# Modulation sums over the partitions: plain fp32, unsplit, the columns halved over the output partitions

## The chip, the cores and the metric

The kernel runs on one core of a Trainium2 chip. Its time is the device time of one execution in microseconds. The kernel before took 1994.59 us (median of three runs, 1993.12 to 1994.67). A profile is one further execution, recorded instruction by instruction; its times begin at the first instruction. Engines are named as in the profile: PE is TensorE (PEld its weight loads), ACT is ScalarE, DVE is VectorE, POOL is GpSimd and SP is the queue that issues most transfers.

## The reference, cut to what matters

One decoder layer on 256 tokens of 2048 channels, all in fp32: an FFN, a mixer (pooling and attention, gated) and a second FFN. Each of the three is modulated by nine vectors that come from the conditioning vector `c`:

```
mod = (silu(c) @ w_ada + b_ada).reshape(9, 2048)      # w_ada: 2048 x 18432
h = rms_norm(x, g) * (1 + mod[1]) + mod[0];  x = x + 0.5 * mod[2] * swiglu(h, ...)   # first FFN
h = rms_norm(x, g) * (1 + mod[4]) + mod[3];  x = x + mod[5] * (merged @ w_o)         # mixer
h = rms_norm(x, g) * (1 + mod[7]) + mod[6];  x = x + 0.5 * mod[8] * swiglu(h, ...)   # second FFN
```

So three of the vectors are shifts, three are scales and three (numbers 2, 5 and 8) are gates.

## The kernel before

**The weight products.** Activations are held transposed, with channels on the 128 partitions and tokens as columns. Each large product has a piece of the activations as its stationary operand (128x128) and 512 weight columns as its moving operand, and sums over the channels in a PSUM bank. Both operands are split into a high and a low half of the type fp32r, and three of the four products are formed (`mm`, the matmuls on L304): 12 matmuls for 128 channels, 1024 columns and both blocks of tokens. The weights are split on the chip as they arrive: ScalarE casts the high half (`wh`, L285, three buffers) and VectorE subtracts it (`wl`, L289).

**Turns.** The order of the work is written out by hand. One "turn" is the matmuls of one weight piece. `push` puts a piece's matmuls off until two more pieces have been prepared (`LAG` is 2), and `at(n, f)` puts `f` behind the matmuls of turn `n`. The planner `spread` places work of a given cost into turns that have room, by the costs booked with `will`; a booked cost changes where later work lands, not the work itself. `hop(n, f, g, early)` puts `f` into turn `n` and `g` into the next, and moves both on past turns at which a column set ends. The eight PSUM banks are two groups of four: one holds the running column set, and `bank()` hands out the other four in turn for all else.

**The modulation sums.** The first two vectors are made at the start, in another way. The other seven are made by `ada_plan`, in 15 blocks spread over the three stages: 13 of 1024 columns and 2 of 512. For one block, VectorE multiplies each piece of `w_ada` (128 rows) by the matching column of silu(c) and adds it to an accumulator `acc` of 128 partitions (L230, 16 operations). The sum over the 128 partitions is then left, and `sums` does it for 512 columns at a time, 28 times in all:

- `halves`, one turn after the last accumulation: ScalarE casts the high half of `acc` (L189), VectorE subtracts for the low half (L190). Both go into buffers of the tag `t2`, of which there are three.
- `prod`, two turns later: two matmuls with a matrix of ones as the stationary operand (L195, L196) give the sums, alike on all 128 output partitions of a bank.
- `use`, in the next turn: for a gate, ScalarE writes the 512 columns into the gate's tile, scaled (L202). For a shift or a scale, `mod_col` takes them to one column for each 128 channels: VectorE multiplies by the identity (L168), reduces (L171) and adds the bias (L175 to L178).

`halves` is booked at 0.65 and `mod_col` at 1.7. The second 512 columns of a block follow the first at least two turns later. The next block starts in the turn in which the last accumulation of the one before stands.

Of the kernel before, what the change touches and what calls it, by code (L numbers as in the profile page):

```python
# [9 lines left out]
F32 = mybir.dt.float32  # L10
F32R = mybir.dt.float32r
BF16 = mybir.dt.bfloat16
AF = mybir.ActivationFunctionType
ALU = mybir.AluOpType
AX = mybir.AxisListType

P = 128
# [12 lines left out]
CW = 512  # L30
# [4 lines left out]
T2 = 3  # L35
# [8 lines left out]
def trunk_layer(ctx, tc, x, c, w_ada, b_ada, g_ffn1, w_ffn1_gu, w_ffn1_down, g_mix, w_in,  # L44
                pool_mix, pool_scale, w_pool_up, q_gain, k_gain, sinks, rel_bias, w_attn_up,
                w_o, g_ffn2, w_ffn2_gu, w_ffn2_down, pool_w, onehot, out):
    nc = tc.nc
    pool = lambda name, bufs=1, **kw: ctx.enter_context(tc.tile_pool(name=name, bufs=bufs, **kw))
    const = pool("const")
# [5 lines left out]
    def nm(s):  # L55
        uid[0] += 1
        return f"{s}_{uid[0]}"

    def t_(shape, tag, bufs=1, dt=F32):
        return sb.tile(list(shape), dt, tag=tag, bufs=bufs, name=nm(tag))  # L60
# [5 lines left out]
    def bank_at(i, shape):  # L66
        return ps.tile(list(shape), F32, tag=f"bank{i}", name=nm("bank"))

    def bank(shape=(P, CW)):
        for _ in range(4):  # L70
            rr[0] = (rr[0] + 1) % 4
            i = (1 - cur[0]) * 4 + rr[0]
            if i not in held:
                return bank_at(i, shape)
        raise RuntimeError("no bank free in the written order")


    ident = const.tile([P, P], F32, name="ident")
    make_identity(nc, ident)
    ones_f = const.tile([P, P], F32, name="ones_f")  # L80
    nc.gpsimd.memset(ones_f, 1.0)
    ones = const.tile([P, P], F32R, name="ones")
    nc.vector.tensor_copy(ones, ones_f)

    x_sb = const.tile([P, T, D], F32, name="x_sb")

# [29 lines left out]
    def at(n, f, first=False):  # L116

        fs = plan.setdefault(max(n, done[0]), [])
        fs.insert(0, f) if first else fs.append(f)
# [4 lines left out]
    def hop(n, f, g, early=0):  # L124


        while n in ends or early > 0 and n + 1 in ends or early > 1 and n - 1 in ends:
            n += 1
        at(n, f)
        at(n + 1, g)  # L130
        return n
# [11 lines left out]
    def spread(n, m, cost, cap=9.0):  # L143

        out, left = [], 0.0
        while len(out) < m:
            r = room.get(n, ROOM)
            left = min(left, 2 * cost) + max(0.0, min(r - busy.get(n, 0.0), r * cap / ROOM))
            while left >= cost and len(out) < m:
                out.append(n)  # L150
                left -= cost
            n += 1
        return out

    def will(n, t):
        busy[n] = busy.get(n, 0.0) + t
# [5 lines left out]
    gates = {}  # L162

    def mod_col(j, b, c0):

        k, n = c0 // P, b.shape[1] // P
        d = t_([P, n, P], "t2", T2)
        nc.vector.tensor_tensor(d, b.rearrange("p (a q) -> p a q", a=n),  # L168
                                ident.unsqueeze(1).to_broadcast([P, n, P]), ALU.mult)
        m = mcol[:, j, k:k + n]  # L170
        nc.vector.tensor_reduce(m, d, AX.X, ALU.add)  # L171
        i, o = j // 3, j % 3
        bc = bcol[:, (2 * i + o) * KD + k:(2 * i + o) * KD + k + n]
        if o == 0:
            nc.vector.tensor_tensor(m, m, bc, ALU.add)  # L175
        else:
            nc.vector.scalar_tensor_tensor(out=m, in0=m, scalar=1.0, in1=bc, op0=ALU.add, op1=ALU.add)
            nc.vector.tensor_tensor(m, m, gcol[:, i * KD + k:i * KD + k + n], ALU.mult)  # L178

    def ada_plan(js, n0, cap=9.0):  # L180

        def sums(j, c0, a, n, o):
            got = []

            def halves():
                hi, lo = t_([P, CW], "t2", T2, F32R), t_([P, CW], "t2", T2, F32R)
                nc.scalar.copy(hi, a[0][:, o:o + CW])  # L189
                nc.vector.tensor_tensor(lo, a[0][:, o:o + CW], hi.bitcast(F32), ALU.subtract)  # L190
                got.extend((hi, lo))

            def prod():
                got.append(bank())
                nc.tensor.matmul(got[2], ones, got[0], start=True, stop=False)  # L195
                nc.tensor.matmul(got[2], ones, got[1], start=False, stop=True)  # L196

            def use():
                if j % 3 == 2:
                    if j not in gates:  # L200
                        gates[j] = t_([P, D], "gate", 1)
                    nc.scalar.activation(gates[j][:, c0 + o:c0 + o + CW], got[2], AF.Copy, scale=1.0 if j == 5 else 0.5)  # L202
                else:
                    mod_col(j, got[2], c0 + o)

            at(n, halves)
            q = hop(n + 2, prod, use, 2)
            will(n, 0.65)
            if j % 3 != 2:
                will(q + 1, 1.7)  # L210
            return q

        for j, c0, a_w in js:
            a, r, nk = [], [], 2 * SW // a_w
            where = spread(n0, KD, 1.24 * a_w / SW, cap)
            for kk, n in enumerate(where):
                def go(j=j, c0=c0, kk=kk, a=a, r=r, w=a_w, nk=nk):
                    if kk == 0:
                        a.append(t_([P, w], "acc", 2))
                        if j % 3 == 2:  # L220
                            nc.gpsimd.memset(a[0], 0.0)
                            nc.gpsimd.dma_start(a[0][0:1, :], b_ada[0:1, j * D + c0:j * D + c0 + w])
                    if kk % nk == 0:
                        r[:] = [t_([P, nk, w], "raw", RAW)]
                        nc.sync.dma_start(r[0], ada_v[:, kk:kk + nk, j * D + c0:j * D + c0 + w])
                    sc = cs[:, kk:kk + 1]
                    if kk == 0 and j % 3 != 2:
                        nc.vector.tensor_scalar_mul(a[0], r[0][:, 0, :], sc)
                    else:
                        nc.vector.scalar_tensor_tensor(out=a[0], in0=r[0][:, kk % nk, :], scalar=sc, in1=a[0],  # L230
                                                       op0=ALU.mult, op1=ALU.add)
                at(n, go)
                will(n, 1.24 * a_w / SW)
            n0 = n
            q = n
            for i in range(a_w // CW):
                q = sums(j, c0, a, max(n + 1 + 2 * i, q + 1), i * CW)


    class Set:  # L240
# [309 lines left out]
    def ffn(w_gu, w_down, hh, hl, actT, f0, sg, g, jgate, after, js):  # L550
# [25 lines left out]
        for i in range(4):  # L576
            will(n + KF - 1 + 2 * i, 1.36)
        ada_plan(js, pushed[0], ROWS)
        while f0 < DFF:
            fw = min(SW, DFF - f0)  # L580
# [41 lines left out]
    for i, g in enumerate((g_ffn1, g_mix, g_ffn2, pool_scale)):  # L622
        n = g.shape[1] // P
# [132 lines left out]
    b = bank_at(4, (P, KG + KB))  # L756
# [48 lines left out]
    for k, n, need in ((2, 4, 14), (6, 4, 42), (10, 4, 70), (14, 2, 74)):  # L805
# [29 lines left out]
        q = k  # L835
        while q < k + n:
            m = 1 if q == k + n - 1 else 2
            if q - q % 2 in xT:
                at(e + (q > k + 1), lambda q=q, m=m: h_pair(xT[q - q % 2][:, q % 2:q % 2 + m, :], q, m))
            else:  # L840
                xn, o = [], (q - k) // 2
# [9 lines left out]
    for i, k0, k1 in segs:  # L851
        s = Set(w_ffn1_gu[0], KD, cols[i], hstat, late=True)
        if n0 == 0:
# [3 lines left out]
            h = t_([P, 2, S], "t2", T2)  # L857
# [213 lines left out]
    for a in range(0, 8, 2):  # L1071
        with_bank(G[0] + 1 + a // 4, (P, 2, S), pool_prod(a),
                  lambda b, a=a: nc.vector.tensor_copy(pT_[0][:, a:a + 2, :], b))
        will(G[0] + 2 + a // 4, 0.7)
    for a in range(8):
        with_bank(G[0] + 4 + a // 2, (P, S), mix_prod(a),
                  lambda b, a=a: nc.scalar.activation(mixT[:, a, :], b, AF.Copy, scale=psc[:, a:a + 1]))
# [100 lines left out]
    for g, n in enumerate((2, 5, 9, 13, 17, 22, 25, 28)):  # L1178
        heads(G[0] + n, g)
    ada_plan([(j, c, SW) for j in (5, 6) for c in (0, SW)] + [(7, CW, CW), (7, SW, SW)], nQ)  # L1180

    tk = [(t, i) for t in range(T) for i in range(2)]
# [19 lines left out]
    for half_ in range(2):  # L1202
        c0 = half_ * SW
# [55 lines left out]
    g, hh, hl = transition(s, SW, 5, 6, lambda stat: Set(w_ffn2_gu[0], KD, (0, SW), stat, flip=False, late=True))  # L1259
# [76 lines left out]
```

## Time and profile before

| | |
|---|---|
| median of three runs | 1994.59 us |
| the profiled execution's own time | 1996.08 us |
| its span, first to last instruction | 1994.3 us |
| TensorE, matmuls | 1972.3 us busy, 8873 records |
| TensorE, weight loads | 1629.3 us busy |
| VectorE | 1513.6 us busy, 1749 instructions |
| ScalarE | 1091.8 us busy, 1484 instructions |
| matmuls of the modulation sums (L195 and L196) | 28 records each |
| splits of the accumulators (L189 on ScalarE, L190 on VectorE) | 28 each, 17.3 and 19.2 us busy |
| gate writes (L202) | 12, 7.1 us busy |
| granted TensorE clock, mean | 0.996 |

A row of the timeline has the start and the time from the first start to the last end in microseconds, the engine, the line and operation, the tile written and those read, the shape, and how many instructions stand together. A matmul's end is modelled and overlaps its follower, so starts are compared with starts. A row of a group has, behind the bar, the busy microseconds, the mean nanoseconds of one, and behind the second bar the engine's idle time just before, with what ended it. A matmul's shape is first that of its stationary operand (128\*64 is 128 rows and 64 columns), then that of its moving operand. In the table by stretches each engine has its busy time and number of instructions (PE, PEld, DVE, ACT, POOL), and then come the granted clock, the busy share of the DMA engines and GB/s.

### The profile page before, as it was taken

The page shows a single profiled execution, that of the slowest core. Times are in us where ns is not written, and L with a number is a line of the kernel's source. Part 1 is how long each engine was busy: PE and PEld are TensorE (multiplying, and loading weights), DVE is VectorE, ACT ScalarE, POOL GpSimd, SP SyncE. Part 2 cuts the span into 40 slices and gives each one's busy share as a digit, 9 for nine tenths or more (in the row PEclk, how much of TensorE's full clock was granted, in tenths as well). Part 3 has the DMA queues.
Part 4 walks back from the last instruction along what each step waited for, and adds up shares of the span by engine and source line. Part 5 has one row for each costly group of instructions (what it writes and reads, how often), then busy time and mean ns, then how long its engine had stood idle before and what let it go on. Part 6 is the DMA issues. An engine that isn't in the chain of part 4 may idle for free.

```text
span 1994.3 us, 23770 instructions
## 1 busy us (share of the span) xinstructions
PE 1972.3 (99%) x8873; PEld 1629.3 (82%) x8873; DVE 1513.6 (76%) x1749; ACT 1091.8 (55%) x1484; POOL 26.4 (1%) x51
## 2 busy tenths in 40 slices
PE   7999999999999999999999999999999999999999
PEld 6788888888788888888788888888888888888887
DVE  6898867989999978886889998888455454565655
ACT  6543457664664546446656455645564645565443
POOL 0000000000000000000000000000000000000000
PEclk9999999999999999999999999999999999999999
DMA  9989745899899966876688996598555645466652
GB/s 364 371 314 342 261 164 187 329 337 356 313 363 336 335 230 235 310 281 219 235 292 302 351 311 219 212 356 317 214 189 202 219 170 190 159 225 216 218 185 74
DMA packets 158212, 523.68 MB, mean 263 GB/s; under 512 B 9325, under 2 KB 21509, under 8 KB 157840
## 3 DMA queue, kind: packets, MB, share of 16 engines
q1 hardware_dynamic: 156464, 518.83, 72.7%
q0 software_dynamic: 1632, 3.34, 0.6%
q8 instruction: 69, 1.13, 0.2%
q14 instruction: 47, 0.39, 0.1%
HBM read 520.00 MB, written 2.12 MB: 262 GB/s over the span
## 4 chain that ended last, share of the span: by engine, by line
PE 96%; DVE 2%; DMA 1%; SPq 0%; issue 0%; ACT 0%; DVEq 0%; ACTq 0%
PE bank L304 93%; DVE acc L662 1%; DMA raw<-in_w_ffn_gu_dram 1%; DMA raw<-in_w_ada_dram 0%; DVE wl L289 0%; PE bank L1065 0%; SPq L654 0%; PE bank L820 0%; PE bank L196 0%; PE bank L195 0%; PE bank L357 0%; PE bank L1128 0%; PE bank L1092 0%; PE bank L999 0%; PE bank L1051 0%
## 5 line engine op out<-in xcount | busy, mean ns | idle before, releaser
L285 ACT CAST wh<-raw 128x1024 fp32r<-128x1024 f32 (+2 forms) x711 | 711.1, 1002 | 793.9 <-PE bank L304 739.7
L289 DVE TENSOR_TENSOR wl<-raw,wh 128x1024 fp32r<-128x1024 f32 (+2 forms) x713 | 823.5, 1157 | 418.4 <-ACT wh L285 413.7
L304 PE MATMUL bank<-wh,hl 128*128 128x512 f32 (+1 forms) x2088 | 653.6, 388 | 0.0
L304 PE MATMUL bank<-wh,hh 128*128 128x512 f32 (+1 forms) x2064 | 651.3, 390 | 0.3 <-DVE big L1099 0.3
L304 PE MATMUL bank<-wl,hh 128*128 128x512 f32 (+1 forms) x2064 | 647.5, 389 | 0.6 <-DVE wl L289 0.6
L304 PEld LDWEIGHTS bank<-wh,hl 128*128 128x128 f32 x2088 | 392.7, 188 | 81.3
L304 PEld LDWEIGHTS bank<-wl,hh 128*128 128x128 f32 x2064 | 388.2, 188 | 82.9 <-DVE wl L289 2.9
L304 PEld LDWEIGHTS bank<-wh,hh 128*128 128x128 f32 x2064 | 386.4, 189 | 80.2 <-issue 0.8
L230 DVE SCALAR_TENSOR_TENSOR acc<-raw,cs,acc 128x1024 f32<-128x1024 f32 (+1 forms) x231 | 279.8, 1211 | 0.8
L304 PE MATMUL bank<-wh,sh 128*128 128x512 f32 x656 | 203.7, 390 | 0.0
L304 PE MATMUL bank<-wh,sl 128*128 128x512 f32 x656 | 203.3, 389 | 0.0
L304 PE MATMUL bank<-wl,sh 128*128 128x512 f32 x656 | 203.1, 389 | 0.0
L304 PEld LDWEIGHTS bank<-wh,sl 128*128 128x128 f32 x656 | 123.0, 188 | 26.0 <-DVE sl L394 0.3
L304 PEld LDWEIGHTS bank<-wl,sh 128*128 128x128 f32 x656 | 123.1, 188 | 25.8
L304 PEld LDWEIGHTS bank<-wh,sh 128*128 128x128 f32 x656 | 122.6, 188 | 25.8 <-issue 0.4
L542 ACT COPY big<-raw 32x512 f32<-32x512 f32 (+1 forms) x208 | 121.9, 586 | 4.2
L662 DVE SCALAR_TENSOR_TENSOR acc<-raw,cs,acc 128x1024 f32<-128x1024 f32 (+2 forms) x74 | 77.7, 1052 | 1.0
L394 DVE TENSOR_TENSOR sl<-big,sh 128x512 fp32r<-128x512 f32 x82 | 56.2, 686 | 0.0
L393 ACT CAST sh<-big 128x512 fp32r<-128x512 f32 x82 | 50.7, 618 | 0.0
L784 DVE TENSOR_TENSOR big<-bank,big 128x512 f32<-128x512 f32 x56 | 36.4, 684 | 0.0
L329 ACT ACTIVATE junk<-x_sb 128x512 bf16<-128x512 f32 x24 | 15.2, 632 | 13.9 <-DVE x_sb L421 11.7
L538 DVE STREAM_TRANSPOSE raw<-sg 128x1024 f32<-128x1024 f32 (+1 forms) x20 | 22.7, 1133 | 0.0
(220 smaller groups left out, 802.7 us busy)
## 6 DMA issues: line engine op xcount, KB each, us to landing
raw<-in_w_ffn_gu_dram SPq DMA_DIRECT2D x175, 1024.0 KB, 5.3
raw<-in_w_ada_dram SPq DMA_DIRECT2D x112, 1024.0 KB, 7.2
raw<-in_w_ffn_down_dram SPq DMA_DIRECT2D x86, 1024.0 KB, 6.1
raw<-in_w_in_dram SPq DMA_DIRECT2D x48, 1024.0 KB, 6.8
raw<-in_w_ada_dram SPq DMA_DIRECT2D x64, 512.0 KB, 7.6
raw<-in_w_o_dram SPq DMA_DIRECT2D x15, 1024.0 KB, 7.8
raw<-in_w_pool_up_dram SPq DMA_DIRECT2D x8, 1024.0 KB, 7.9
raw<-in_w_attn_up_dram SPq DMA_DIRECT2D x8, 1024.0 KB, 6.9
```

Of the source, the lines that this page charges most:

```text
L230: nc.vector.scalar_tensor_tensor(out=a[0], in0=r[0][:, kk % nk, :], scalar=sc, in1=a[0], op0=ALU.mult, op1=ALU.add)
L285: nc.scalar.copy(wh, raw_k)
L289: nc.vector.tensor_tensor(wl[:, e], raw_k[:, e], wh[:, e].bitcast(F32), ALU.subtract)
L304: nc.tensor.matmul(self.banks[t][i], a[:, sl], w[:, o], start=first and q == 0, stop=last and q == 2)
L329: nc.scalar.activation(junk, x_sb[:, t, n * CW:(n + 1) * CW], AF.Square, scale=(D / 2) ** -0.5, accum_out=ssq[:, t, n:n + 1])
L393: nc.scalar.copy(hi, src[:, k:k + n, :])
L394: nc.vector.tensor_tensor(lo, src[:, k:k + n, :], hi.bitcast(F32), ALU.subtract)
L538: nc.vector.transpose(z[0][:, t, :], (src() if callable(src) else src)[:, t, 0:n])
L542: nc.scalar.copy(actT[32 * j:32 * j + 32, k:k + m, :].rearrange("p k (t i r) -> p k t i r", t=T, i=4)[:, :, :, i, :], z[0][32 * i:32 * i + ...
L662: nc.vector.scalar_tensor_tensor(out=acc, in0=r, scalar=sc, in1=acc, op0=ALU.mult, op1=ALU.add)
L784: nc.vector.tensor_tensor(a, b, a, ALU.add)
```

## The change

A block's sum over the partitions is formed in one go, for all of its columns, from the unsplit fp32 accumulator. There are two plain fp32 matmuls with 64 columns of ones: one sums one half of the block's columns into output partitions 0 to 63, the other sums the other half into partitions 64 to 127 of the same bank. For a gate the halves are the first and the last columns of the block; for a shift or scale they are the first and the last 64 of every 128. `halves` is gone. `prod` stands two turns after the last accumulation instead of three.

For a shift or a scale, `mod_col` works once on a bank of 512 columns for a block of 1024 (256 for one of 512), with a 128x64 pattern `ident2`, the two halves of the identity added, in place of the identity. For a gate, each half is written twice, once to either half of the gate's partitions: four ScalarE operations of 64 partitions. Of the costs booked, 0.65 is gone and 1.7 for 512 columns becomes 1.4 for a block of 1024 columns (0.75 for one of 512).

```
@@ -79,8 +79,8 @@
     make_identity(nc, ident)
     ones_f = const.tile([P, P], F32, name="ones_f")
     nc.gpsimd.memset(ones_f, 1.0)
-    ones = const.tile([P, P], F32R, name="ones")
-    nc.vector.tensor_copy(ones, ones_f)
+    ident2 = const.tile([P, 64], F32, name="ident2")
+    nc.vector.tensor_tensor(ident2, ident[:, 0:64], ident[:, 64:P], ALU.add)
 
     x_sb = const.tile([P, T, D], F32, name="x_sb")
 
@@ -163,10 +163,11 @@
 
     def mod_col(j, b, c0):
 
-        k, n = c0 // P, b.shape[1] // P
-        d = t_([P, n, P], "t2", T2)
+
+        k, n = c0 // P, 2 * b.shape[1] // P
+        d = t_([P, n, 64], "t2", T2)
         nc.vector.tensor_tensor(d, b.rearrange("p (a q) -> p a q", a=n),
-                                ident.unsqueeze(1).to_broadcast([P, n, P]), ALU.mult)
+                                ident2.unsqueeze(1).to_broadcast([P, n, 64]), ALU.mult)
         m = mcol[:, j, k:k + n]
         nc.vector.tensor_reduce(m, d, AX.X, ALU.add)
         i, o = j // 3, j % 3
@@ -181,34 +182,34 @@
 
 
 
-        def sums(j, c0, a, n, o):
+        def sums(j, c0, a, n, w):
             got = []
 
-            def halves():
-                hi, lo = t_([P, CW], "t2", T2, F32R), t_([P, CW], "t2", T2, F32R)
-                nc.scalar.copy(hi, a[0][:, o:o + CW])
-                nc.vector.tensor_tensor(lo, a[0][:, o:o + CW], hi.bitcast(F32), ALU.subtract)
-                got.extend((hi, lo))
-
             def prod():
-                got.append(bank())
-                nc.tensor.matmul(got[2], ones, got[0], start=True, stop=False)
-                nc.tensor.matmul(got[2], ones, got[1], start=False, stop=True)
+
+                got.append(bank((P, w)))
+                for g in range(2):
+                    if j % 3 == 2:
+                        m = a[0][:, g * w:(g + 1) * w]
+                    else:
+                        m = a[0].rearrange("p (a h r) -> p a h r", h=2, r=64)[:, :, g, :]
+                    nc.tensor.matmul(got[0][64 * g:64 * g + 64], ones_f[:, 0:64], m, start=True, stop=True)
 
             def use():
                 if j % 3 == 2:
                     if j not in gates:
                         gates[j] = t_([P, D], "gate", 1)
-                    nc.scalar.activation(gates[j][:, c0 + o:c0 + o + CW], got[2], AF.Copy, scale=1.0 if j == 5 else 0.5)
+                    for g in range(2):
+                        c_ = c0 + g * w
+                        for r in range(0, P, 64):
+                            nc.scalar.activation(gates[j][r:r + 64, c_:c_ + w], got[0][64 * g:64 * g + 64],
+                                                 AF.Copy, scale=1.0 if j == 5 else 0.5)
                 else:
-                    mod_col(j, got[2], c0 + o)
-
-            at(n, halves)
-            q = hop(n + 2, prod, use, 2)
-            will(n, 0.65)
+                    mod_col(j, got[0], c0)
+
+            q = hop(n, prod, use, 2)
             if j % 3 != 2:
-                will(q + 1, 1.7)
-            return q
+                will(q + 1, 0.1 + 1.3 * w / CW)
 
         for j, c0, a_w in js:
             a, r, nk = [], [], 2 * SW // a_w
@@ -232,9 +233,7 @@
                 at(n, go)
                 will(n, 1.24 * a_w / SW)
             n0 = n
-            q = n
-            for i in range(a_w // CW):
-                q = sums(j, c0, a, max(n + 1 + 2 * i, q + 1), i * CW)
+            sums(j, c0, a, n + 2, a_w // 2)
 
 
     class Set:
```

## The prediction

> **What bounds the kernel now.** I read the page first, for the busy shares.
>
> ```profile
> PE 1972.3 (99%) x8873; PEld 1629.3 (82%) x8873; DVE 1513.6 (76%) x1749; ACT 1091.8 (55%) x1484; POOL 26.4 (1%) x51
> ```
>
> TensorE has no room: 8873 matmul records in a span of 1994.3 us. A busy share can overstate a pipelined engine, so the chain of waits in order of time came next. Its longest piece is the last quarter of the kernel.
>
> ```profile
> 1415.51 573.96 PE bank L304 x2532
> ```
>
> There the chain is nothing but weight matmuls (L304), each starting 573.96 / 2532 = 0.2267 us after the one before. This is the pace of the kernel wherever nothing interrupts it; every microsecond put into or taken out of TensorE's queue moves the end by as much. The view of waits says who waits for whom.
>
> ```profile
> ACT wh L285 <- PE bank L304: 739.7, 544, 5.4
> ```
>
> ScalarE's casts of the weights wait 739.7 us in total for TensorE to free their buffers: the preparing engines run ahead and are held back by TensorE. Work taken off ScalarE or VectorE is worth nothing except where TensorE is caught waiting for them. So the change is priced in TensorE's queue first, and then at the places where it waits.
>
> **The change, part by part.** The kernel makes 15 blocks of modulation sums inside the three big stages: 13 of 1024 columns and 2 of 512, by the lists handed to the planner.
>
> *Removed: the fp32r product.* Each 512 columns have two matmuls (L195, L196), one for either half of the split. TensorE's timeline around one such sum:
>
> ```profile
> 414.19 0.39 PE L304 MATMUL bank<-wh,hl 128*128 128x512 f32 x1
> 414.42 0.62 PE L304 MATMUL bank<-wl,hh 128*128 128x512 f32 x2
> 414.88 0.39 PE L195 MATMUL bank<-t,ones 128*128 128x512 f32 x1
> 415.11 0.40 PE L196 MATMUL bank<-t,ones 128*128 128x512 f32 x1
> 415.34 0.62 PE L304 MATMUL bank<-wh,hh 128*128 128x512 f32 x2
> 415.80 0.39 PE L304 MATMUL bank<-wh,hl 128*128 128x512 f32 x1
> ```
>
> From 414.19 to 415.80 are 1.61 us with five L304 starts and the sum: 1.61 - 5 x 0.2267 = 0.48 us for a sum. There are 28, so 0.96 us for a wide block, 0.48 us for a narrow one, and 13.4 us in all.
>
> *Added: two plain fp32 matmuls a block, one to either half of the output partitions.* No sum in the trace has that form, but two neighbours do. A full-width plain fp32 product is L1065, of 256 columns:
>
> ```profile
> 895.96 1.89 PE L1065 MATMUL bank<-sg,raw 128*128 128x256 f32 x8
> 897.50 0.58 PE L195 MATMUL bank<-t,ones 128*128 128x512 f32 x1
> 897.92 0.40 PE L196 MATMUL bank<-t,ones 128*128 128x512 f32 x1
> 898.16 0.63 PE L304 MATMUL bank<-wh,hh 128*128 128x512 f32 x2
> ```
>
> From 895.96 to 898.16 are 2.20 us; without the sum's 0.48 that is 1.72 us for 8 records, 0.215 us each. That is nearly the 0.2267 us of an L304 record with twice the columns, so a plain fp32 record costs 1.9 times as much per column. I take 0.43 us for 512 columns. Plain fp32 also doubles the records. The attention's output product (L1161) has 8 calls in the code, one to either half of the partitions for each of four groups of heads and one of the two blocks, and the groups of matmuls show 16:
>
> ```profile
> L1161 PE MATMUL bank<-sg,big 128*64 128x256 f32 x16 | 2.6, 404 | 0.0
> ```
>
> So a block of 1024 columns gets four records of 0.43 us, 1.72 us if they follow one another. Whether the two halves share the time decides the case. L1161, with L1158 and L1159 behind it, is the one place with 128x64 weights and both halves of one bank:
>
> ```profile
> 957.90 0.61 PE L304 MATMUL bank<-wl,sh 128*128 128x512 f32 x2
> 958.45 0.65 PE L1161 MATMUL bank<-sg,big 128*64 128x256 f32 x4
> 958.93 0.65 PE L1158 MATMUL bank<-sg,big 128*64 128x256 f32 x4
> 959.36 0.65 PE L1159 MATMUL bank<-sg,big 128*64 128x256 f32 x4
> 959.94 0.73 PE L304 MATMUL bank<-wh,sh 128*128 128x512 f32 x2
> 960.51 0.39 PE L304 MATMUL bank<-wh,sl 128*128 128x512 f32 x1
> ```
>
> The twelve records begin at 958.45 and the next L304 at 959.94: 1.49 us, where one after another they need 12 x 0.215 = 2.58. The halves do run side by side, six pairs in 6 x 0.215 = 1.29 us. From 957.90 to 960.51 are 2.61 us; less four L304 starts (0.91) that is 1.70 us, so 0.41 us go to the passage. It splits thus: 0.10 us of waiting on the way in (958.45 against 957.90 + 2 x 0.2267), 0.05 us in the first four records (0.48 against 0.43), 0.15 us behind the last four (0.58 against 0.43), 0.11 us in the second L304 after. The 0.15 holds the lag of one half behind the other; a block's sum has only the first group's four records, so I take 0.10 there, and 0.36 us in all, with 0.41 as the other end.
>
> A wide block then costs 2 x 0.43 + 0.36 = 1.22 us, 0.26 more than now; a narrow one 0.43 + 0.36 = 0.79, 0.31 more. Sum: 13 x 0.26 + 2 x 0.31 = **+4.0 us on TensorE**; with 0.41 it is +4.8 us.
>
> On the order of the records a page speaks against the change. The Trainium skill, TensorE: Matmul & The Clock Gate, Part 3 (The mechanism), says that matmuls keep strict program order in start and end. By that rule, with both records of one half written ahead of the other half's, only the middle two could overlap, and a wide block would take three record times instead of two. The twelve records above, written in such an order, would by it fill nine record times, 1.94 us; the trace has 1.49 us to the next L304, so I keep to the trace and leave the rule a rival.
>
> *Removed: the splitting, and half of the column work.* VectorE's groups:
>
> ```profile
> L190 DVE TENSOR_TENSOR t<-acc,t 128x512 fp32r<-128x512 f32 x28 | 19.2, 686 | 1.3 <-ACT t L189 1.2
> ...
> L171 DVE TENSOR_REDUCE mcol<-t 128x4 f32<-128x512 f32 x16 | 11.0, 686 | 0.6
> ...
> L168 DVE TENSOR_TENSOR t<-bank,ident 128x512 f32<-128x512 f32 x16 | 11.0, 685 | 0.0
> ```
>
> L190 goes: 19.2 us. L168 and L171 run 16 times at 1.37 us together; afterwards 9 times, at most at that price, 9.6 us saved or more. About 29 us leave VectorE. ScalarE:
>
> ```profile
> L189 ACT CAST t<-acc 128x512 fp32r<-128x512 f32 x28 | 17.3, 619 | 4.4 <-DVE acc L230 4.3
> ...
> L202 ACT ACTIVATE gate<-bank 128x512 f32<-128x512 f32 x12 | 7.1, 594 | 2.5 <-PE bank L196 2.5
> ```
>
> L189 goes (17.3 us). The gates grow: six gate blocks write four 64-partition pieces instead of two whole ones, 12 more of L202. I price a piece of 64 partitions like one of 128, 0.59 us (half of that is the other end), so +7.1 us. All of this lies under TensorE's work. What it can give back is where TensorE waits, and the table by stretches of time has one such stretch, in the narrow last column set of the first FFN, whose turns are half as long:
>
> ```profile
> 498.00:528.00 30.00, 29.73 (x127) 23.11 (x127) 27.52 (x41) 22.14 (x36) 0.00 (x0) 1.00 0.85 312
> ```
>
> 127 matmuls at 0.2267 are 28.8 us of 30: 1.2 us lost, give or take one matmul at the edges, with VectorE busy for 27.52. A sum now puts about 2 x (0.69 + 1.37) = 4.1 us on VectorE; afterwards 1.4. But the planner's costs fall too, so that it books the next block's accumulations into the freed turns. I take **-0.8 us**, between -1.2 (all of it) and +1.2 (the earlier accumulations hit these short turns worse).
>
> *Moved: the product one turn earlier, the columns after it.* It now waits directly for the last accumulation, not for the split. Behind it on TensorE wait the next turn's L304. The accumulation is two turns ahead, about 2 x 12 x 0.2267 = 5.4 us in a wide set, which covers an operation of 1.3 us; in the narrow set half of that. I price it at nothing there, the +1.2 above being what it costs without the cover. The buffer of the accumulator is now freed by the product; two take turns, so the block after next waits for it, some 16 turns later: nothing. The transfers that follow move with the accumulations, by a turn or two, in the same order and number; the casts' wait for TensorE shows that they come early enough.
>
> *At the start.* The constant changes on VectorE:
>
> ```profile
> 1.12 0.43 DVE L83 CAST ones<-ones_f 128x128 fp32r<-128x128 f32 x1 [1.12 <-POOL ones_f L81]
> 12.35 0.49 DVE L660 TENSOR_SCALAR acc<-raw,cs 128x512 f32<-128x512 f32 x1 [10.80 <-DMA raw<-in_w_ada_dram]
> ```
>
> The addition that replaces it has 10.8 us of idle time behind it. Nothing.
>
> **Sum.** +4.0 - 0.8 = **+3.2 us**. The profiled execution took 1996.08 us (span 1994.3 and 1.8 around it) and would take 1999.3; the median of the three runs lies 1.5 us lower, 1994.59, so the forecast is **1997.8 us**, +0.16%.
>
> **The rivals.** *A gate's bank held too long (slower).* The two blocks for the gate of the mixer are made during the attention, where banks are taken quickly and ScalarE is busy with the exponentials. The sum of 897.50, quoted above, got its gate only here:
>
> ```profile
> 901.54 0.58 ACT L202 ACTIVATE gate<-bank 128x512 f32<-128x512 f32 x1
> 902.02 1.03 ACT L285 CAST wh<-raw 128x1024 fp32r<-128x1024 f32 x1
> ...
> 902.73 0.71 PE L1092 MATMUL bank<-big 64*128 64x256 f32 x4
> ...
> 903.09 1.23 DVE L289 TENSOR_TENSOR wl<-raw,wh 128x1024 fp32r<-128x1024 f32 x1 [3.68 <-ACT wh L285]
> ...
> 908.03 0.81 PE L304 MATMUL bank<-wh,hh 128*128 128x512 f32 x2
> ```
>
> Four pieces instead of one end at 901.54 + 4 x 0.59 = 903.9, 1.8 us later. The weights cast behind them, at 902.02, are used from 908.03 and their low half is ready at 904.3, so 3.7 us of cover remain. But four banks go round, and the logits at 902.73 (L1092) can be the next to want this one: a wait of up to 903.9 - 902.73 = 1.2 us, and as much again at the second block: +3.2 + 2.4 = +5.6 us, **2000.2 us**. It decides from 0.8 us of such waiting on. Against it: the sum may land in a quieter turn, and a bank is only wanted after three others.
>
> *The passage costs its other end:* +4.8 and no gain from the stalls, **1999.4 us**, just slower.
>
> *The halves do not overlap as in L1161:* three record times instead of two are 13 x 0.43 + 2 x 0.215 = 6.0 us more, **2003.8 us**; none at all, twice that, 2009.8 us. Against it stands 1.49 us for twelve records. (The three record times are what the order rule in the Trainium skill, TensorE: Matmul & The Clock Gate, would make of it.)
>
> *Faster:* the passage at 0.36, all of the 1.2 us back, and other small waits gone would still be +2.8. To end 4 us below, the shifted plan would have to clear about 7 us of waiting, and the stretch above, where VectorE is fullest, holds 1.2. That the relief of VectorE and ScalarE shortens the kernel by more than I see, **1990 us**, keeps a small chance.
>
> **How the numbers follow.** Forecast 0.48; bank held 0.17; dearer passage 0.18; overlap failing 0.08; faster 0.09. A measurement of this kernel tells about 0.2% (4 us) from no change, so 1990.6 to 1998.6 is "same". Of the forecast's own cases (its range is 1995 to 2000) about a tenth of all the chance lies above 1998.6, and of the rivals on the slow side about as much lies below: same 0.50, slower 0.42, faster 0.08. The range reaches from 1993.0 (the stalls gone and a passage below 0.36) to 2003.0, short of the case where the overlap fails.
>
> **What would show it.** Right: 60 records of form 128*64 on the new line, starting in pairs; about 1.2 us between the weight matmuls before and after a block; L189 and L190 gone; 24 pieces of L202; VectorE about 29 us and ScalarE about 10 us less busy, with the chain of waits still almost all L304. Wrong: records one after another (2 us and more a block), a matmul waiting for a gate, for the accumulator or for the columns' reading, a lower granted clock, or the stretch around 500 to 530 us losing more than now.

## The result, and the profile after

The changed kernel takes **1998.99 us** (median of 13 runs, 1997.22 to 2000.08), the kernel before 1994.53 us (13 runs beside it, 1992.86 to 1995.34). The ratio is 1.0023, 95% interval 1.0015 to 1.0030: 4.5 us slower. The forecast was 1997.8 us in a range of 1993.0 to 2003.0; the time lies in the range, and just past the 0.2% that the forecast called "same". One run of an experiment (5147 us) and one of the kernel before beside another (2193 us) lie far outside all others and are left out of the ratios.

The head of the page, profile after:

```profile
PE 1977.2 (99%) x8877; PEld 1622.1 (81%) x8877; DVE 1486.3 (74%) x1697; ACT 1083.5 (54%) x1468; POOL 26.3 (1%) x51
```

TensorE has four records more (60 for the sums in place of 56). VectorE has 27.3 us less to do and ScalarE 8.3, and the kernel is slower: where TensorE is the bound, relief elsewhere does not count as such.

TensorE's timeline around a sum of 1024 columns, and around one of 512:

```profile
410.12 0.61 PE L303 MATMUL bank<-wl,hh 128*128 128x512 f32 x2
410.67 1.08 PE L196 MATMUL bank<-acc,ones_f 128*64 128x512 f32 x4
411.68 0.73 PE L303 MATMUL bank<-wh,hh 128*128 128x512 f32 x2
412.25 0.39 PE L303 MATMUL bank<-wh,hl 128*128 128x512 f32 x1
...
707.03 0.61 PE L303 MATMUL bank<-wl,sh 128*128 128x512 f32 x2
707.58 0.65 PE L196 MATMUL bank<-acc,ones_f 128*64 128x256 f32 x4
708.16 0.73 PE L303 MATMUL bank<-wh,sh 128*128 128x512 f32 x2
708.73 0.39 PE L303 MATMUL bank<-wh,sl 128*128 128x512 f32 x1
```

From 410.12 to 412.25 are 2.13 us; less four weight matmuls of 0.2267 us that is 1.22 us. The narrow one takes 1.70 - 0.91 = 0.79 us. Both are the forecast's figures. In the queue that is 13 x 0.26 + 2 x 0.31 = 4.0 us; 3.9 with the starts read to the nanosecond.

So the queue explains nearly all of the 4.5 us, but the waits changed too, and they do not cancel by design. The stretch of the narrow column set, in the table by stretches (PE, PEld, DVE, ACT, POOL, clock, DMA share, GB/s):

```profile
498.00:528.00 30.00, 30.00 (x132) 23.93 (x132) 26.82 (x36) 21.79 (x33) 0.00 (x0) 1.00 0.91 330
```

132 records in the place of 127 (the four of the sum cost a little more than four weight matmuls): the 1.2 us of waiting are gone. Two waits are new. In the attention, at the second block for the mixer's gate (TensorE, then ScalarE):

```profile
983.92 0.82 PE L1127 MATMUL bank<-ident,big 128*128 128x128 f32 x6
984.66 0.70 PE L1091 MATMUL bank<-big 64*128 64x256 f32 x2
985.20 0.38 PE L1092 MATMUL bank<-big 64*128 64x128 f32 x2
985.86 0.70 PE L1091 MATMUL bank<-big 64*128 64x256 f32 x2 [0.28 <-ACT gate L205]
986.39 0.38 PE L1092 MATMUL bank<-big 64*128 64x128 f32 x2
986.70 0.73 PE L303 MATMUL bank<-wh,hh 128*128 128x512 f32 x2
987.27 0.40 PE L303 MATMUL bank<-wh,hl 128*128 128x512 f32 x1
```

```profile
983.41 2.39 ACT L205 ACTIVATE gate<-bank 64x512 f32<-64x512 f32 x4
985.83 1.04 ACT L284 CAST wh<-raw 128x1024 fp32r<-128x1024 f32 x1
```

The second head's logits (the second L1091 row) wait for the last of the four gate pieces, which ends at 985.80: 983.41 + 2.39. The same stretch of the kernel before, where no gate is written:

```profile
982.68 0.82 PE L1128 MATMUL bank<-ident,big 128*128 128x128 f32 x6
983.43 0.71 PE L1092 MATMUL bank<-big 64*128 64x256 f32 x4
983.96 0.39 PE L1093 MATMUL bank<-big 64*128 64x128 f32 x4
984.29 0.73 PE L304 MATMUL bank<-wh,hh 128*128 128x512 f32 x2
984.86 0.63 PE L304 MATMUL bank<-wh,hl 128*128 128x512 f32 x2
```

From the transposes to the third weight matmul it takes 984.86 - 982.68 = 2.18 us before and 987.27 - 983.92 = 3.35 us now: **+1.2 us**, at one block of two. The second head starts 1.2 us behind the first (985.86 against 984.66), but TensorE stands idle for only about 0.3 us of it (0.28 in the row). The rest is a lost overlap: before, the logits of both heads together (four records in each row) take 0.86 us, from 983.43 to 984.29, and now the second head's alone take 0.84 us, from 985.86 to 986.70, after the first's.

And weights come late where the transfers are dense, in the first FFN's second product and in the mixer's first pooled product (the profile after, TensorE; the columns as above):

```profile
555.85 0.73 PE L303 MATMUL bank<-wh,hh 128*128 128x512 f32 x2
557.20 0.73 PE L303 MATMUL bank<-wh,hl 128*128 128x512 f32 x2 [0.61 <-DVE hl L393]
```

```profile
1093.62 0.73 PE L303 MATMUL bank<-wh,sh 128*128 128x512 f32 x2
1094.96 0.74 PE L303 MATMUL bank<-wh,sl 128*128 128x512 f32 x2 [0.61 <-DVE sl L393]
```

VectorE is named: it makes the low half of the activations (`hl`, `sl`). But the high half for it stands on ScalarE behind the cast of a weight piece, and that cast waited for a transfer:

```profile
554.23 1.05 ACT L284 CAST wh<-raw 128x1024 fp32r<-128x1024 f32 x1 [5.05 <-DMA raw<-in_w_ffn_down_dram]
```

Near 1094 us the same cast waited 3.83 us for `w_pool_up`. The two rows are 1.35 and 1.34 us apart where two records take 0.45: 0.9 us each.

### The profile page after: what moved, and what is told of

It reads as the page before. It is cut to its first block, busy times and chain, and to the rows that moved or that the text cites. A ratio compares the mean times of both kernels' runs of the same rounds, so it can differ in the third digit from the quotient of the medians.

```text
span 1998.3 us, 23696 instructions
## 1 busy us (share of the span) xinstructions
PE 1977.2 (99%) x8877; PEld 1622.1 (81%) x8877; DVE 1486.3 (74%) x1697; ACT 1083.5 (54%) x1468; POOL 26.3 (1%) x51
```

## The experiments

The theory after the result: the queue costs 3.9 us, and the rest is waits that came and went because the planner's costs, and with them the places of the accumulations and sums, moved. Each time is a median beside the kernel before on the same chip (1994.6 to 1994.7 us).

**The changed product with the plan of before.** After a block the old costs are booked at the old turns; the order of transfers on SP is then the one of before.

```
-            q = hop(n, prod, use, 2)
-            if j % 3 != 2:
-                will(q + 1, 0.1 + 1.3 * w / CW)
+            hop(n, prod, use, 2)
+            p = q = n - 2
+            for i in range(2 * w // CW):
+                m = max(p + 1 + 2 * i, q + 1)
+                q = clear(m + 2)          # hop's turn, nothing placed
+                will(m, 0.65)
+                if j % 3 != 2:
+                    will(q + 1, 1.7)
```

> The changed product and the changed reading, but the planner books the costs of before (0.65 and 1.7 for each 512 columns, at the old turns), so that every accumulation and every transfer of the weights stands where it stood before the change. Theory (TensorE's queue plus a moved plan): the queue still pays 13 x 0.25 + 2 x 0.31 = 3.9 us, the two waits for late weights near 556 and 1094 us (1.0 us each in the changed kernel) are gone, and the old wait near 505 to 526 us (1.6 us) is smaller or gone, since VectorE has less to do: 1996.8 to 1998.4 us, against 1994.5 before and 1999.0 changed. Rival (the late weights are chance, the plan is worth nothing): 1999.0 us, with waits of that kind in some place.

1997.92 us, ratio 1.0013 (1.0003 to 1.0022): +3.3 us by the medians and 2.6 by the ratio, inside the theory's span, and each wide sum takes 1.22 us. The waits near 985 and 1094 us are gone. But the one near 555 is not: here it is even longer, 1.8 us, so it can come without the moved accumulations.

```profile
553.90 0.61 PE L313 MATMUL bank<-wl,hh 128*128 128x512 f32 x2
555.29 0.73 PE L313 MATMUL bank<-wh,hh 128*128 128x512 f32 x2 [0.78 <-ACT hh L402]
556.63 0.73 PE L313 MATMUL bank<-wh,hl 128*128 128x512 f32 x2 [0.61 <-DVE hl L403]
```

**The split sums with the changed plan.** Only the bookings of the change, in the kernel before.

```
-            will(n, 0.65)
-            if j % 3 != 2:
-                will(q + 1, 1.7)
...
             n0 = n
+            if j % 3 != 2:
+                will(clear(n + 2) + 1, 0.1 + 1.3 * (a_w // 2) / CW)
```

> The kernel before, with its split sums, but the changed bookings, so that accumulations and transfers stand where the change puts them. Theory: nothing is added to TensorE's queue, but the waits near 556 and 1094 us appear (1.0 us each): 1995.5 to 1996.5 us. Rival (the plan is worth nothing): 1994.5 us and no such waits.

1995.18 us, ratio 1.0005 (0.9996 to 1.0014): not told from no change. The waits of 556 and 1094 us are absent, against the expectation. The narrow column set's waiting is now nearly all in one place, 1.1 us:

```profile
511.94 0.39 PE L308 MATMUL bank<-wh,hl 128*128 128x512 f32 x1
513.23 0.50 PE L308 MATMUL bank<-wl,hh 128*128 128x512 f32 x1 [0.89 <-DVE wl L293]
```

In the kernel before the largest single wait there was 0.4 us, but the stretch as a whole did not get worse: from 498 to 528 us there are 128 matmuls against 127. New waits stand elsewhere: 0.4 and 0.5 us near 582 and 585 us, where VectorE is busy without a gap, and 0.6 us near 983 us, where a sum waits for a bank.

The late transfers near 1094 us, however, are made by the plan alone. With the changed bookings two pieces of `w_ada` stand in a row on the queue ahead of the weights `w_pool_up`; in the kernel before one of each follows the other (SP's queue and ScalarE's cast of the piece in question, this run and then the kernel before in its second profile):

```profile
1068.97 1.56 SPq L227 DMA_DIRECT2D raw<-in_w_ada_dram  x2
1073.63 0.37 SPq L265 DMA_DIRECT2D raw<-in_w_pool_up_dram  x1
```

```profile
1087.93 1.05 ACT L289 CAST wh<-raw 128x1024 fp32r<-128x1024 f32 x1 [2.79 <-DMA raw<-in_w_pool_up_dram]
```

```profile
1066.71 0.37 SPq L225 DMA_DIRECT2D raw<-in_w_ada_dram  x1
1067.90 0.37 SPq L261 DMA_DIRECT2D raw<-in_w_pool_up_dram  x1
```

```profile
1084.43 1.05 ACT L285 CAST wh<-raw 128x1024 fp32r<-128x1024 f32 x1
```

The low half of the activations behind this cast is ready 0.26 us before TensorE's use here (1090.85 against 1091.11), and 3.2 us before it in the kernel before (1087.34 against 1090.51). So the plan eats the cover, and TensorE escapes by a hair in this profile. The two pieces in a row, and casts of `w_pool_up` that wait 1.7 to 3.8 us for the transfer between 1070 and 1096 us, are in all four profiles with the changed bookings, and in none with the bookings of before.

**Plain fp32 over the full width.** No split, no halving:

```
-                nc.tensor.matmul(got[2], ones, got[0], start=True, stop=False)
-                nc.tensor.matmul(got[2], ones, got[1], start=False, stop=True)
+                nc.tensor.matmul(got[0], ones_f, a[0][:, o:o + CW], start=True, stop=True)
```

> The kernel before without the split: one plain fp32 matmul with 128 columns of ones for each 512 columns, plan and reading as before. Theory: two records of 0.43 us for each of 28 sums instead of 0.48 us, no passage: 28 x 0.38 = +10.6 us on TensorE, less up to 1.6 us of waiting near 505 to 526 us, so 2003.5 to 2005.1 us, and the halving over the output partitions is worth about 6.5 us. Rival (the passage into and out of the half-width form eats what the sharing saves): 1999 us.

2004.88 us, ratio 1.0055 (1.0043 to 1.0068): +10.2 us, as the theory has it. A sum of 512 columns:

```profile
413.20 0.62 PE L296 MATMUL bank<-wl,hh 128*128 128x512 f32 x2
413.66 1.02 PE L189 MATMUL bank<-acc,ones_f 128*128 128x512 f32 x2
414.12 1.04 PE L296 MATMUL bank<-wh,hh 128*128 128x512 f32 x2
414.99 0.62 PE L296 MATMUL bank<-wh,hl 128*128 128x512 f32 x2
```

From 413.20 to 414.99 are 1.79 us; less four weight matmuls (0.91) that leaves 0.88: two records of 0.43 and next to nothing around them. Two such sums are 1.77 us. The halving brings a wide block from 1.77 to 1.22 us, and the 0.36 of passage belong to the half-width form, not to fp32.

**Shifts and scales alone.** The gates summed and written as before, the plan of before.

> The change for shifts and scales alone; the three gates are summed and written as before, and the planner books the costs of before. Theory: 7 x 0.25 + 2 x 0.31 = 2.4 us on TensorE, less up to 1.6 us of waiting: 1995.3 to 1996.9 us, 1.5 us below the kernel with the changed product everywhere and the same plan. Rival (the four gate writes on ScalarE hold banks or casts up): 3 us or more below it.

1996.20 us, ratio 1.0006 (0.9997 to 1.0015), 1.7 us below the run with the gates changed as well; the theory had 1.5 for six sums less. The agreement is partly luck. A wait of 1.3 us for the logits' addition, against 0.47 before, was new here near 965 us (it comes back below), and the intervals overlap. Among runs of equal granted clock (see the last section) the two are 0.2 to 1.1 us apart, with two to four runs on either side. The rival's loss of 3 us by the gates is not seen; a small one is not excluded.

**The three profiles once more.** The changed kernel, the changed product with the plan of before, and the kernel before.

> The changed kernel once more, for its profile. If the waits for late weights near 556 and 1094 us belong to the change's plan, both are there again at the same places with about 1.0 us each. If they are chance in a stretch where the transfers are just fast enough (DMA share 0.96 to 0.99 there), at least one is gone or elsewhere, and the modulation sums still take 1.22 us each.

> The changed product with the bookings of before once more, for its profile, which had 1.9 us of late weights near 555 us. If the place is set by the order of the work, the wait is there again; if it is chance, it is gone or of another size.

> The kernel before once more, for its profile. If the 1.6 us of waiting between 505 and 518 us come from VectorE's load by the sums, they are there again; the stretch from 545 to 560 us shows whether the kernel before can miss its weights there too (then 1 us or more of waiting, as chance would have it; none if only the change brings it).

The late weights near 555 us are gone in both repeats. In the changed kernel the stretch now runs without a gap:

```profile
545.00:560.00 15.00, 15.00 (x68) 12.43 (x67) 13.49 (x14) 9.41 (x15) 0.00 (x0) 1.00 1.00 383
```

The DMA share is 1.00 (0.97 and 0.98 in the two profiles of the kernel before): the transfers are just fast enough there. The same kernel misses a turn in one profile and not in the next, so here it is chance. The wait near 985 us is there again with the same 1.2 us (transposes at 982.79, third weight matmul at 986.14), so it belongs to the changed order. The one near 1094 us is there again with 0.9 us. The kernel before has its wait between 498 and 528 us again (127 records in the same 30 us) and none near 555.

**Two of the four gate pieces on VectorE.** In the changed kernel, for the mixer's gate:

```
+                            if j == 5 and r:
+                                nc.vector.tensor_copy(gates[j][r:r + 64, c_:c_ + w], got[0][64 * g:64 * g + 64])
+                                continue
```

> The changed kernel, but of the mixer's gate the two pieces for partitions 64 to 127 are written by VectorE instead of ScalarE, so that a gate's bank is held for two ScalarE operations instead of four. Theory (the second pair of logits near 985 us waits for the fourth gate piece, which costs 1.2 us there in both profiles of the changed kernel): that wait is gone, since the bank is free about 1.2 us earlier, and the median falls by about 1 us against the changed kernel, to 1997.8 us; the wait near 1094 us stays. Rival (the wait is for ScalarE's or VectorE's other work): it stays within 0.3 us, 1999 us.

1998.92 us, ratio 1.0023 (1.0014 to 1.0032): the time did not move, and the wait is still there. The last piece is now on VectorE, and the wait follows it there:

```profile
983.22 0.38 PE L1095 MATMUL bank<-big 64*128 64x128 f32 x2
984.13 0.70 PE L1094 MATMUL bank<-big 64*128 64x256 f32 x2 [0.53 <-DVE gate L206]
```

```profile
981.43 0.57 ACT L208 ACTIVATE gate<-bank 64x512 f32<-64x512 f32 x1
982.75 0.59 ACT L208 ACTIVATE gate<-bank 64x512 f32<-64x512 f32 x1 [0.75 <-DVE gate L206]
```

The pieces did not run side by side: ScalarE's second waited for VectorE's first. So the bank was held as long as before (from 981.43 to 984.07, where VectorE's second piece ends), and the cure failed; that the logits wait for the last gate piece, whoever writes it, is shown. What a bank freed earlier would be worth was not tested. The wait near 1094 us shrank to 0.3 us in this profile (1091.84 to 1092.58 for two starts), which makes its size, at least, a matter of when the transfers land.

**A quarter of the columns to each quarter of the partitions.** The full-width and half-width sums pointed to a version under the kernel before: the shifts and scales with 32 columns of ones, the gates left as they were.

```
-                for g in range(2):
+                for g in range(4):
-                    nc.tensor.matmul(got[0][64 * g:64 * g + 64], ones_f[:, 0:64], m, start=True, stop=True)
+                    nc.tensor.matmul(got[0][32 * g:32 * g + 32], ones_f[:, 0:32], m, start=True, stop=True)
```

> Shifts and scales summed in plain fp32 with 32 columns of ones, a quarter of the block's columns to each quarter of the output partitions; gates as before; bookings of before. Theory (the streaming halves again, the passage of 0.36 us stays): a wide block of shifts or scales takes 0.43 + 0.36 = 0.79 us instead of 0.97, a narrow one 0.215 + 0.36 = 0.58 instead of 0.48, so 7 x -0.18 + 2 x 0.09 = -1.1 us on TensorE, and up to 1.6 us less of waiting: 1992 to 1993.6 us, the first version below the kernel before. Rival (only two groups of columns run side by side): 1.22 us a wide block, as in the halved form, 1996.2 us.

1994.22 us, ratio 0.9993 (0.9984 to 1.0002). A wide sum:

```profile
503.61 0.39 PE L335 MATMUL bank<-wl,hh 128*128 128x512 f32 x1
503.93 0.64 PE L227 MATMUL bank<-acc,ones_f 128*32 128x256 f32 x8
504.50 0.50 PE L335 MATMUL bank<-wh,hh 128*128 128x512 f32 x1
504.84 0.39 PE L335 MATMUL bank<-wh,hl 128*128 128x512 f32 x1
```

504.84 - 503.61 less two weight matmuls is 0.78 us; a narrow sum, read in the same way near 721 us, is 0.56 us. Both are as expected: eight records run four at a time, and the passage is the same as for halves. The wait near 963 us is here too, 1.3 us against 0.47 before. I put it down to the order in which the four free banks go round, which the smaller number of sums shifts: the next column set first needs the bank of the second pair of logits instead of the first.

```
+                if 4 * w > CW:
+                    rr[0] = (rr[0] + 1) % 4       # pass over one bank
```

> The quartered form with one bank of the round passed over before each wide sum, so that the banks are handed out in the attention as in the kernel before. Theory (the 1.3 us that TensorE waits for the logits' addition near 963 us in the quartered form, against 0.47 us before, come from the order in which the banks go round): that wait is 0.47 us again, and the median falls by 0.8 us against the quartered form, to 1993.2 to 1993.6 us, about 1.3 us below the kernel before. Rival (the wait comes from VectorE being later there): 1.3 us of waiting and the quartered form's time.

> The quartered form once more, timed beside the one with the shifted round. Theory: 1994.2 us and 1.3 us of waiting for the logits' addition near 963 us, with 0.78 us for each wide sum.

The profile with the shifted round, and the one without:

```profile
964.61 0.39 PE L337 MATMUL bank<-wh,hh 128*128 128x512 f32 x1
965.30 0.50 PE L337 MATMUL bank<-wh,hh 128*128 128x512 f32 x1 [0.30 <-DVE big L1132]
```

```profile
962.43 0.61 PE L335 MATMUL bank<-wl,sh 128*128 128x512 f32 x2
964.20 0.70 PE L335 MATMUL bank<-wh,hh 128*128 128x512 f32 x2 [1.15 <-DVE big L1130]
```

The wait changed as the theory said (0.69 us between two starts against 1.77 for two records). The medians do not show it: 1993.36 us (0.9992, 0.9983 to 1.0001) with the shift, 1992.67 us (0.9990, 0.9981 to 0.9999) without. But the two sets of runs had different granted clocks (see the last section). Sorted afterwards by it, the runs do show the gain: at 1.0 the three with the shift took 1990.4 to 1990.7 us, the five without (both sets) 1990.9 to 1991.6; at 0.996 four took 1993.3 to 1993.6 and five 1994.2 to 1994.9. That is about the 0.8 us expected. By the medians the quartered form is 0.5 to 2 us faster than the kernel before, and only one of the three comparisons excludes no change; at a clock of 1.0, where the kernel before takes 1993.2 us, it is 1.9 us faster without the shift and 2.8 with it.

## Why the prediction was right, point by point

- **The two matmuls: right to the tenth.** The halves run side by side, fp32 has two records for a call, a record of 512 columns takes 0.43 us, the passage 0.36 us. 1.22 and 0.79 us were forecast and measured. The rivals of failing overlap and of the dearer passage (0.41) fall; the rule of strict order in the Trainium skill (TensorE: Matmul & The Clock Gate, Part 3) would have given 3 x 0.43 + 0.36 = 1.65 us for a wide block, and the trace does not have it. For quarters the overlap holds fourfold.
- **The relief of the other engines: right in kind, near in size.** VectorE -27.3 us against -29 forecast, ScalarE -8.3 against -10. A gate piece of 64 partitions costs as much as one of 128 (0.594 us before), as this group of the profile after shows:

```profile
L205 ACT ACTIVATE gate<-bank 64x512 f32<-64x512 f32 x24 | 14.2, 593 | 2.5 <-PE bank L196 2.3
```

- **The stalls: the term was mis-sized, too small in its own place and without two others.** -0.8 was taken for the narrow column set; there it was -1.2, the forecast's best end, and it is absent from every profile whose sums are not split. The other bound, that earlier accumulations make this stretch worse, was seen in no profile. Where the split sums stayed, the earlier accumulations cost waits elsewhere, near 582, 585 and 983 us. And the term counted one place only: the waits near 985 and 1094 us, 2.1 us together, were not in it.
- **The transfers "in the same order and number", and so early enough: wrong.** I read from the casts' large wait for TensorE, a sum over the whole kernel, that weights come early enough everywhere. In the stretches near 555 and 1094 us the DMA share is at 1.0 and weights miss their turn by up to 0.9 us, by chance in the one. In the other the order did change: two pieces of `w_ada` go ahead of the weights in every profile with the changed bookings, and TensorE waits 0.9, 0.9 and 0.3 us in the three of them that have the changed sums.
- **"A gate's bank held too long": a rival, and it happened as well.** Place, mechanism and price (1.2 us) were as written, at one of the two blocks instead of both. The first block's sum fell ahead of the attention, at 870 us.
- **The sum.** 3.9 in the queue, -1.2 in the narrow set, +1.2 at the gate's bank, +0.9 near 1094 us, and up to 0.9 more by chance near 555: 4.8 to 5.7 us by places, against 4.5 measured. The forecast's +3.2 missed the two waits, which together took back more than the relief of VectorE gave. Three profiles have the same granted clock, 0.999: the changed kernel with the wait near 555 us (span 1998.3 us), without it (1996.9) and the kernel before (1992.5). They lie 5.8 and 4.4 us apart, as the sum by places says. That the total came within 1.2 us of the forecast is partly luck: 2.1 us of waits were not in its sum, and 0.5 us less than taken in the narrow set and in the queue set a part of them off. The rival of the dearer passage, at 1999.4 us, was nearer in number and wrong in its cause.

What stays open: how often the changed kernel misses the turn near 555 us, with two profiles of it, and what a plan without the two pieces in a row near 1070 us would give with the halved sums. The nearest to it, the changed product with the plan of before, has no wait near 1094 us, nor near 985 us, and costs 3.3 us against 4.5 by the medians.

## What to carry to other kernels

A product whose output partitions are all alike can be spread over parts of the output partitions: here halves took 1.22 us and quarters 0.78 us for 1024 fp32 columns where the full width took 1.77, and the passage in and out was about 0.36 us in either form, to be weighed against the streaming saved. It pays only if the form it replaces is dearer: the two split pairs in fp32r took 0.96. In a kernel bound by one engine, price a change in that engine's queue first, and then look for the three things that a moved plan can turn into waits: dense transfers, banks that go round, and a reader that now needs four operations instead of one to give a bank back.

## What the runs showed of the hardware that I had not expected

Near 70 us most profiles have a few microseconds at half the clock (granted clock 0.50 from 67.5 to 73.5 us in the kernel before), as the weight products begin, but not equally many, and three show none there. The stretch from 70 to 80 us of the kernel before, and of the quartered form's second profile:

```profile
70.00:80.00 10.00, 10.00 (x37) 8.05 (x36) 6.92 (x7) 6.21 (x8) 3.37 (x8) 0.80 0.96 340
```

```profile
70.00:80.00 10.00, 10.00 (x43) 8.23 (x42) 8.45 (x9) 5.79 (x8) 2.95 (x7) 0.93 1.03 373
```

The mean clock is 0.80 in one and 0.93 in the other, and six matmuls more are done: 1.4 us that no edit made. The record has the granted clock of each run, and it sorts the times. Of the runs of the kernel before beside the experiments, 22 with a clock of 1.0 took 1993.0 to 1993.9 us, 35 with 0.999 took 1994.5 to 1997.8 (median 1994.7), and 11 with 0.996 took 1996.1 to 1998.9. The two groups of the 13 runs above, near 1993.2 and near 1994.6 us, are about where the first two lie. Against runs of equal clock the changed kernel is 4.3 us slower, at 1.0 (2 runs) as at 0.999 (10 runs). Differences under a microsecond in this kernel are to be read from the places in the trace, or from runs of equal granted clock, not from the medians alone.
